# Loads pinned, stores on another queue, two units made earlier and slots shifted in a one-core hybrid layer

## The chip, the cores and the metric

The kernel runs on one core of one Trainium2 chip. The metric is the device time of one execution in microseconds (us). Matrix products run on TensorE (PE in the profile, its weight loads PEld), element-wise work on VectorE (DVE) and ScalarE (ACT), a little of it on GpSimd (POOL). SyncE (SP) only issues DMAs. ScalarE and GpSimd issue DMAs too. An engine runs its instructions, DMA issues among them, in one fixed order, and a waiting instruction holds up all that stand behind it.

## The reference

One decoder layer on 512 tokens of width 2048, with 16 meta tokens ahead of them, in float32:

```
u = rmsnorm(h, norm_mix);  proj = u @ w_in
mix = concat(attention(proj), mlstm(proj) * gate)
h = h + mix @ w_out                                     # 2048 x 2048
u = rmsnorm(h, norm_mlp)
h = h + square(relu(u @ w_up)) @ w_down                 # 2048 x 8192, 8192 x 2048
return rmsnorm(h, norm_final)
```

The change lies in the last column block of `w_out`, in the product with `w_up` and at the start of the product with `w_down`.

## The kernel before, in words

**Split products.** Each float32 operand is split into a high half in fp32r and the remainder. ScalarE makes the high half (the cast at L121), VectorE subtracts it from the source (L122), and TensorE takes three products: high x high, high x low, low x high. In the names, `whi` and `wlo` are the halves of a weight (three buffers each), and tiles `s0` to `s15` of `xpool` are slots that hold high and low halves of activations side by side. A slot is 2 x 528 numbers wide (`TOK` is 528). `xpair(i, 512)` uses 2 x 512 of them, from the slot's start if `i` is even and 32 numbers (128 bytes) later if it is odd.

**w_out (L838 to L914).** Four blocks of 512 columns, j = 0 to 3. For each, four 1 MB weight tiles come through two buffers (`raw_tile`, L134), 512-row products run at L714 to L716, VectorE adds the residual rows (`hs`, L869), the rows are stored to DRAM (`hd`, L873), transposed by TensorE (L878) and turned into the seven combinations of rows that the next product uses. Their squares are summed by ScalarE (L707). The rows tile has two buffers, so blocks 2 and 3 use one each.

**w_up (`up_quad`, L746 to L834).** The product is done in 32 quads of hidden units by a fast 2x2 scheme with seven products instead of eight. A quad loads two 1 MB raw tiles (L753): even quads into the two buffers of `raw_tile`, odd quads into two buffers of a pool `b2r` that lies where the tiles of the w_out loop were. `x11`, `x12`, `x21`, `x22` are its quarters. VectorE makes the sums s1 to s4 (L744, three buffers, `NS_`), `operand` splits a quarter or a sum, and `product` runs 24 matmuls (8 blocks of k, three each, L764 to L766) for it. From quad 1 on the order of products is x11, x12, s2, s1, s3, s4, x22. The activations of the scheme are `yh[p, j]`, `yl[p, j]`: for j below 2 in tiles of their own (`y`), for j = 2 and 3 in slots 0 to 13 (two for each p). Quad 0 is begun inside the last block of w_out by `first_quad`. At the end of a quad come square, four sums `fs` (L829 to L832, on VectorE, for the last quad on GpSimd) and two stores to `fdram` (L833, L834).

**w_down (from L986).** It reads the activations back as 512-number "units" (`load_unit`, L950), in the order of `keys_`, and splits each into a slot (`split_unit`): unit k goes to slot `XU[k]`, so units 0 and 1 go to slots 14 and 15, which w_up leaves free, and units 2 and 3 to slots 0 and 1, which hold rows of the first product. Units 0 and 1 are made early, in quads 4 and 5 (`early_unit`). `load_units` and `next_units` keep five loads ahead (`FB`). The products (L1068 to L1072) run in 16 blocks of 14 steps of 12 matmuls. A step needs its weight operand, its units and now and then a difference of weight tiles (`weight_sum`, L1037).

**Order.** Tile's scheduler orders each engine's instructions by a simulation of the program. Inside `manual_schedule` (for w_down: TensorE, ScalarE and VectorE) the written order is kept. Before its first product w_down writes: operands 0 and 1, the first half of `t1`, and `next_units(3)`, so units 2, 3 and 4. Then step 0: the second half of `t1`, operand 2, one unit.

Of the kernel before, what the change touches and what calls it, by code (L numbers as in the profile page):

```python
# [11 lines left out]
F32R = mybir.dt.float32r  # L12
# [5 lines left out]
P = 128  # L18
# [5 lines left out]
TOK = META + SEQ  # L24
# [15 lines left out]
NQ = FF // P // 2  # L40
HTOK = SEQ // 2
NS_ = 3
FB = 5
# [40 lines left out]
def hybrid_layer(ctx, tc, io, out):  # L84
# [15 lines left out]
        return aps.tile(list(shape), F32, tag="a", name="a")  # L100


    def xpair(i, n, dt=F32R):
        t = xpool.tile([P, 2 * TOK], dt, tag=f"s{i}", name=f"s{i}")
        o = (TOK - n) * (i % 2) * 2
        return t[:, o : o + 2 * n].rearrange("p (a n) -> p a n", a=2)

    cst = cpool.tile([P, C_N], F32, name="cst")
    act.dma_start(out=cst[:, :KT], in_=io["cst"][:, :KT])
# [613 lines left out]
    b2 = b2s.enter_context(tc.tile_pool(name="b2", bufs=1, reuse_waits="tile"))  # L723
    yh, yl = {}, {}

    def y_pair(p, j, t):
        t = t.rearrange("p a (q n) -> p a q n", q=2)
        yh[p, j], yl[p, j] = t[:, 0], t[:, 1]

    for p in ORDER:  # L730
        for j in range(2):
            y_pair(p, j, b2.tile([P, 2, 512], F32R, name=f"y{p}_{j}")[:])

    def sum_tile():
        return b2.tile([P, 1024], F32, name="s", tag="s", bufs=NS_)


    def operand(src):
        w = hi_lo()
        split(w[0][:], w[1][:], src)  # L740
        return w
# [4 lines left out]
    def up_quad(quad):  # L746
        raws = []
        for i in range(2):
            if quad % 2:
                raw = b2r.tile([P, 2048], F32, name=f"raw{i}")  # L750
            else:
                raw = raw_tile()
            sync.dma_start(out=raw[:], in_=io["w3"][quad, i])  # L753
            raws.append(raw)
        x11, x12 = raws[0][:, :1024], raws[0][:, 1024:]
        x22, x21 = raws[1][:, :1024], raws[1][:, 1024:]
        s1, s2, s3, s4 = (sum_tile() for _ in range(4))
        nb = abank if quad % 2 else bank

        def product(p, w, out, q0=0, q1=KQ, start=True):  # L760
            for q in range(q0, q1):
                wh, wl = (t[:, q * P : (q + 1) * P] for t in w)
                ah_, al_ = yh[p, q // 2][:, q % 2], yl[p, q // 2][:, q % 2]
                pe.matmul(out, wh, ah_, start=start and q == 0, stop=False, skip_group_check=True)  # L764
                pe.matmul(out, wh, al_, start=False, stop=False, skip_group_check=True)  # L765
                pe.matmul(out, wl, ah_, start=False, stop=q == KQ - 1, skip_group_check=True)  # L766

        if quad == 0:
            pa, pb, pc = (nb((P, 2, HTOK)) for _ in range(3))
            pd = nb((P, HTOK))  # L770
            pp2, pp6 = pd[:], pa[:, 1]
            w_sum(s1, x21, x22, ALU.add)
            w_sum(s2, s1[:], x11, ALU.subtract)
            w_sum(s4, x12, s2[:], ALU.subtract)
            early = [(p, operand(src), o) for p, src, o in ((0, x11, pa[:, 0]), (1, x12, pp2), (2, s4[:], pc[:, 1]))]
            yield
            product(*early[0], 0, 2)
            yield
            for (p, w, o), q0 in zip(early, (2, 0, 0)):
                product(p, w, o, q0, KQ - 2)  # L780
            yield
            for p, w, o in early:
                product(p, w, o, KQ - 2, KQ)
            product(4, operand(s1[:]), pb[:, 1])
            product(3, operand(x22), pc[:, 0])
            w_sum(s3, x11, x21, ALU.subtract)
            product(6, operand(s3[:]), pb[:, 0])
            product(5, operand(s2[:]), pp6)

            d = b2b.tile([P, 4, HTOK], F32, name="d", bufs=2)  # L790
            v = b2b.tile([P, 4, HTOK], F32, name="fs")
            sb, u2, u = v[:, 2], v[:, 3], v[:, :2]
            act.copy(sb, pa[:, 0])
            dve.tensor_tensor(out=d[:, 0], in0=sb, in1=pp2, op=ALU.add)
            dve.tensor_tensor(out=u2, in0=sb, in1=pp6, op=ALU.add)
            dve.tensor_tensor(out=u, in0=v[:, 3:].to_broadcast([P, 2, HTOK]), in1=pb[:], op=ALU.add)
            dve.tensor_tensor(out=d[:, 3], in0=u[:, 0], in1=pb[:, 1], op=ALU.add)
            dve.tensor_tensor(out=d[:, 1:3], in0=u, in1=pc[:], op=ALU.add)
            act.activation(d[:], d[:], AF.Relu)
        else:  # L800

            X, B = nb((P, HTOK)), nb((P, 2, HTOK))
            W, Q = B[:, 0], B[:, 1]
            d = b2b.tile([P, 4, HTOK], F32, name="d", bufs=2)
            product(0, operand(x11), X[:])
            act.copy(d[:, 0], X[:])
            w_sum(s1, x21, x22, ALU.add)
            w_sum(s2, s1[:], x11, ALU.subtract)
            product(1, operand(x12), W)
            product(5, operand(s2[:]), X[:], start=False)  # L810
            dve.tensor_tensor(out=d[:, 0], in0=d[:, 0], in1=W, op=ALU.add)  # L811
            act.copy(d[:, 2], X[:])
            product(4, operand(s1[:]), Q)
            w_sum(s3, x11, x21, ALU.subtract)
            act.copy(d[:, 1], Q)
            product(6, operand(s3[:]), X[:], start=False)
            w_sum(s4, x12, s2[:], ALU.subtract)
            act.copy(d[:, 3], X[:])
            product(2, operand(s4[:]), Q, start=False)
            dve.tensor_tensor(out=d[:, 3], in0=d[:, 3], in1=d[:, 1], op=ALU.add)  # L820
            act.activation(d[:, 0], d[:, 0], AF.Relu)
            product(3, operand(x22), X[:], start=False)
            dve.tensor_tensor(out=d[:, 2], in0=d[:, 2], in1=Q, op=ALU.add)
            act.activation(d[:, 2:4], d[:, 2:4], AF.Relu)
            act.activation(d[:, 1], X[:], AF.Relu)
        act.activation(d[:], d[:], AF.Square)
        fs = b2b.tile([P, 4, HTOK], F32, name="fs")
        summer = dve if quad < NQ - 1 else pool
        summer.tensor_tensor(out=fs[:, 0], in0=d[:, 2], in1=d[:, 3], op=ALU.add)  # L829
        summer.tensor_tensor(out=fs[:, 1], in0=fs[:, 0], in1=d[:, 0], op=ALU.subtract)  # L830
        summer.tensor_tensor(out=fs[:, 2], in0=d[:, 2], in1=d[:, 0], op=ALU.subtract)
        summer.tensor_tensor(out=fs[:, 3], in0=d[:, 1], in1=fs[:, 1], op=ALU.subtract)  # L832
        act.dma_start(out=fdram[quad // 2][0][:, :, quad % 2], in_=d[:])  # L833
        (act if quad < NQ - 1 else pool).dma_start(out=fdram[quad // 2][1][:, :, quad % 2], in_=fs[:])  # L834
# [3 lines left out]
    with tc.tile_pool(name="b2a", bufs=1, reuse_waits="tile") as b2a:  # L838
        for j in range(NJ):
# [30 lines left out]
                        out=hs[b][:], in0=ps[b][:], scalar=sc[:, b : b + 1], in1=hs[b][:], op0=ALU.mult, op1=ALU.add  # L870
                    )
            for b in range(NB):
                sync.dma_start(out=hd[j][b // 2][:, b % 2], in_=hs[b][:])  # L873
            ts = [abank((P, NB, P)) for _ in range(4)]

            def transposes(i, bs):
# [18 lines left out]
                act.activation(y[:, i], src, AF.Copy, scale=gmlp[:, kt : kt + 1])  # L895
            if j >= 2:
                for i, p in enumerate(ORDER):
                    y_pair(p, j, xpair(2 * i + j - 2, 512))
            y11, y12 = y[:, 0:2, :HTOK], y[:, 0:2, HTOK:]
            y21, y22 = y[:, 2:4, :HTOK], y[:, 2:4, HTOK:]  # L900
            t1, t2, t4 = (b2a.tile([P, 2, HTOK], F32, name=f"t{i}")[:] for i in range(3))
# [45 lines left out]
    def load_unit(k, buf):  # L947
        c, p, h = keys_[k]
        pos = FPOS.index(p)
        sync.dma_start(out=buf[:].rearrange("p (a b) -> p a b", a=2), in_=fdram[2 * c + h][pos // 4][:, pos % 4])  # L950

    def split_unit(k, buf):
        unit[keys_[k]] = hi, lo = unit_pair(k)
        split(hi, lo, buf[:])
# [42 lines left out]
    def load_units(n):  # L997
        for k in range(len(loaded), min(n, len(keys_))):
            loaded[k] = f_buffer()
            load_unit(k, loaded[k])  # L1000

    def next_units(n):
        for k in range(len(unit), min(len(unit) + n, len(keys_))):
            load_units(k + FB)
            split_unit(k, loaded[k])
# [191 lines left out]
        last_sq[b] = b3.tile([P, 1], F32, name=f"sq{b}")  # L1197
        act.activation(junk, h1[b, j], AF.Square, accum_out=last_sq[b][:])

    load_units(FB)  # L1200
    load_rows0(0, 0)
    load_rows0(0, 1)
    load_rows1(0)
# [1 line left out]
    with tc.manual_schedule(engines={mybir.EngineType.PE, mybir.EngineType.Activation, mybir.EngineType.DVE}):  # L1205
        weight_operand(0)
        weight_operand(1)
        weight_sum(0, "t1", 0)
        next_units(3)
        for g in range(LAST):  # L1210
            product(g)
            step(g)
            if g == LAST - STEPS + 2:
                load_nf()
            elif g == LAST - STEPS + 8:
                for j in range(NJ):
                    act.activation(nfs[j][:], nfs[j][:], AF.Copy, scale=float(D) ** 0.5)

        for row, j in ((0, 3), (1, 2)):
            b = slice(2 * row, 2 * row + 2)  # L1220
            pool.tensor_scalar(out=ssh[:, b, j], in0=epss[:, b], scalar1=float(D), scalar2=None, op0=ALU.mult)
        for m in range(STEPS - 2):
            product(LAST + m)
            last_step(m)
# [89 lines left out]
```

## Time and profile before

| | |
|---|---|
| median of three runs | 1988.95 us (1987.78 to 1991.22) |
| the profiled execution | 1988.79 us, its span 1987.0 us |
| granted TensorE clock, mean | 0.997 |
| bytes read from and written to HBM | 244.45 MB, 78.15 MB |

The profile is of one execution. Its span goes from the first to the last instruction. Times of day in the text are microseconds from the span's start. In a row of a timeline stand start, duration, engine, line, operation, tile written and tiles read, shapes and count; in brackets follows how long the engine had been idle before it and what ended that. Rows close together and alike are merged, so that a duration can be that of several. The rows of TensorE overlap, since matmuls are pipelined: the distance of their starts tells the pace.

### The profile page before, as it was taken

How to read it: one execution, taken by the hardware profiler on the slowest of the kernel's cores; microseconds unless marked ns; L12 is line 12 of the kernel's file. 1: busy time of each engine (PE TensorE's matmuls, PEld its weight loads, DVE VectorE, ACT ScalarE, POOL GpSimd, SP SyncE). 2: the span in 40 equal slices, each digit the busy share in tenths (PEclk: the TensorE clock that was granted, in tenths of full speed). 3: DMA queues.
4: the chain of work that ended last, by engine and by line, in shares of the span. 5: the costliest groups of instructions: out<-in, count | busy, mean ns of one | idle time of the engine just before them, and what ended most of it. 6: DMA issues, size and time to landing. Idle time of an engine off the chain costs nothing.

```text
span 1987.0 us, 30628 instructions
## 1 busy us (share of the span) xinstructions
PE 1964.6 (99%) x12240; PEld 1759.7 (89%) x12240; DVE 1407.7 (71%) x1844; ACT 1011.8 (51%) x1491; POOL 226.0 (11%) x342
## 2 busy tenths in 40 slices
PE   9999999999999999999999999999999999999997
PEld 7878889988888889999999999998888888888885
DVE  6547773233644478777777787778898898888888
ACT  4433542235533355555555555556566666655655
POOL 0112220012120021222210000001100010010010
PEclk9999999999999999999999999999999999999999
DMA  8412112211343346555554454547888887787866
GB/s 315 132 64 87 64 65 86 85 69 64 107 155 139 107 148 215 180 188 175 186 180 160 149 170 149 170 149 230 225 223 213 232 216 211 227 216 201 220 173 189
DMA packets 113008, 324.61 MB, mean 163 GB/s; under 512 B 14016, under 2 KB 50496, under 8 KB 93904
## 3 DMA queue, kind: packets, MB, share of 16 engines
q1 hardware_dynamic: 66304, 246.60, 36.5%
q0 software_dynamic: 12000, 40.90, 10.7%
q10 hardware_dynamic: 34560, 35.14, 5.5%
q8 instruction: 96, 1.57, 0.3%
q14 instruction: 48, 0.39, 0.1%
HBM read 244.45 MB, written 78.15 MB: 162 GB/s over the span
## 4 chain that ended last, share of the span: by engine, by line
PE 68%; issue 24%; POOL 3%; DVE 2%; DMA 2%; ACT 1%; SPq 0%; POOLq 0%; DVEq 0%; ACTq 0%
PE g L168 10%; PE a L766 5%; PE a L765 5%; PE a L764 5%; PE g L764 5%; PE g L765 5%; PE g L766 5%; PE g L714 3%; PE g L716 3%; PE g L715 3%; PE g L231 2%; PE g L183 2%; POOL hd L1078 2%; PE g L181 2%; PE g L182 2%
## 5 line engine op out<-in xcount | busy, mean ns | idle before, releaser
L121 ACT CAST whi<-raw 128x1024 fp32r<-128x1024 f32 x224 | 234.9, 1049 | 409.1 <-PE g L716 85.5
L122 DVE TENSOR_TENSOR wlo<-raw,whi 128x1024 fp32r<-128x1024 f32 x224 | 274.7, 1227 | 206.4 <-ACT whi L121 201.4
L122 DVE TENSOR_TENSOR wlo<-s,whi 128x1024 fp32r<-128x1024 f32 x256 | 313.4, 1225 | 119.9 <-ACT whi L121 117.6
L121 ACT CAST whi<-s 128x1024 fp32r<-128x1024 f32 x256 | 268.9, 1051 | 223.1 <-PE a L765 67.1
L168 PE MATMUL g<-s,whi 128*128 128x264 f32 x1216 | 205.0, 287 | 0.2 <-DVE qa L267 0.2
L168 PEld LDWEIGHTS g<-s,whi 128*128 128x128 f32 x1216 | 170.9, 189 | 5.4 <-issue 4.9
L1068 PE MATMUL X<-whi,s 128*128 128x512 f32 x356 | 138.5, 389 | 0.0
L1071 PE MATMUL X<-wlo,s 128*128 128x512 f32 x356 | 138.5, 389 | 0.0
L1072 PE MATMUL X<-whi,s 128*128 128x512 f32 x356 | 138.5, 389 | 0.0
L764 PE MATMUL g<-y,whi 128*128 128x256 f32 x448 | 127.2, 284 | 1.3 <-ACT whi L121 1.1
L764 PE MATMUL a<-y,whi 128*128 128x256 f32 x448 | 127.0, 284 | 1.5 <-DVE d L811 1.0
L168 PE MATMUL g<-s,wlo 128*128 128x264 f32 x608 | 128.0, 287 | 0.0
L766 PE MATMUL a<-y,wlo 128*128 128x256 f32 x448 | 127.0, 283 | 0.6 <-DVE wlo L122 0.6
L764 PE MATMUL a<-s,whi 128*128 128x256 f32 x448 | 126.8, 283 | 0.0
L765 PE MATMUL a<-s,whi 128*128 128x256 f32 x448 | 126.8, 283 | 0.0
L766 PE MATMUL a<-s,wlo 128*128 128x256 f32 x448 | 126.8, 283 | 0.0
L766 PE MATMUL g<-y,wlo 128*128 128x256 f32 x448 | 126.8, 283 | 0.0
L765 PE MATMUL g<-y,whi 128*128 128x256 f32 x448 | 126.8, 283 | 0.0
L765 PE MATMUL a<-y,whi 128*128 128x256 f32 x448 | 126.8, 283 | 0.0
L765 PE MATMUL g<-s,whi 128*128 128x256 f32 x448 | 126.7, 283 | 0.0
L766 PE MATMUL g<-s,wlo 128*128 128x256 f32 x448 | 126.7, 283 | 0.0
L764 PE MATMUL g<-s,whi 128*128 128x256 f32 x448 | 126.5, 283 | 0.0
(368 smaller groups left out, 5114.4 us busy)
## 6 DMA issues: line engine op xcount, KB each, us to landing
raw<-in_w_dram SPq DMA_DIRECT2D x144, 1024.0 KB, 5.1
rh<-in_w_dram SPq DMA_DIRECT2D x64, 512.0 KB, 5.6
hd<-c POOLq DMA_DIRECT2D x61, 512.0 KB, 5.5
fu<-fd SPq DMA_DIRECT2D x110, 256.0 KB, 3.7
fd<-d ACTq DMA_DIRECT2D x32, 512.0 KB, 3.2
fd<-fs ACTq DMA_DIRECT2D x31, 512.0 KB, 3.5
xtok<-in_x_dram SPq DMA_DIRECT2D x4, 1024.0 KB, 11.6
hs<-in_x_dram SPq DMA_DIRECT2D x16, 256.0 KB, 6.1
```

What stands on the lines that cost most here:

```text
L121: act.copy(dst_hi, src)
L122: dve.tensor_tensor(out=dst_lo, in0=src, in1=dst_hi.bitcast(F32), op=ALU.subtract)
L168: pe.matmul(ps[s][:], w, x[:, s * HALF : (s + 1) * HALF], start=first and kt == 0, stop=last and kt == KT - 1,)
L714: pe.matmul(ps[b][:], a, wh, start=kt == first, stop=False)
L715: pe.matmul(ps[b][:], a, wl, start=False, stop=False)
L716: pe.matmul(ps[b][:], c, wh, start=False, stop=kt == last)
L764: pe.matmul(out, wh, ah_, start=start and q == 0, stop=False, skip_group_check=True)
L765: pe.matmul(out, wh, al_, start=False, stop=False, skip_group_check=True)
L766: pe.matmul(out, wl, ah_, start=False, stop=q == KQ - 1, skip_group_check=True)
L1068: pe.matmul(out[:, t], a, wh[:, cols], start=start and h == q == 0, stop=False, skip_group_check=True)
L1071: pe.matmul(out[:, t], a, wl[:, cols], start=False, stop=False, skip_group_check=True)
L1072: pe.matmul(out[:, t], a2, wh[:, cols], start=False, stop=h == q == 1, skip_group_check=True)
```

## The change

- `xslot` returns a whole slot, and `y_pair` takes the first 1024 numbers of a tile. The w_up rows (j = 2, 3) in odd slots therefore start at the slot's start instead of 128 bytes later. Units keep `xpair`.
- In quad 2 both raw loads are kept in program order on SyncE, so they are issued behind everything that the program has put on that queue before, quad 1's loads among it.
- The row stores of the last block of w_out (four of 256 KB) are issued by GpSimd instead of SyncE.
- In the last quad (31) a tile `u` of the sum tiles' ring takes the loads of units 2 and 3, and the two are split behind the second product in the program's text. w_down starts with four units made: it loads units 4 to 8 ahead, and makes one unit (4) instead of three before its first product.

```diff
+    def xslot(i, dt=F32R):
+        return xpool.tile([P, 2 * TOK], dt, tag=f"s{i}", name=f"s{i}")
+
     def xpair(i, n, dt=F32R):
-        t = xpool.tile([P, 2 * TOK], dt, tag=f"s{i}", name=f"s{i}")
         o = (TOK - n) * (i % 2) * 2
-        return t[:, o : o + 2 * n].rearrange("p (a n) -> p a n", a=2)
+        return xslot(i, dt)[:, o : o + 2 * n].rearrange("p (a n) -> p a n", a=2)
...
-    def y_pair(p, j, t):
-        t = t.rearrange("p a (q n) -> p a q n", q=2)
+    def y_pair(p, j, t, o=0):
+        t = t[:, o : o + 1024].rearrange("p (a q n) -> p a q n", a=2, q=2)
         yh[p, j], yl[p, j] = t[:, 0], t[:, 1]
...
-            y_pair(p, j, b2.tile([P, 2, 512], F32R, name=f"y{p}_{j}")[:])
+            y_pair(p, j, b2.tile([P, 1024], F32R, name=f"y{p}_{j}"))
...
-            sync.dma_start(out=raw[:], in_=io["w3"][quad, i])
+            load = sync.dma_start(out=raw[:], in_=io["w3"][quad, i])
+            if quad == 2:
+                tc.keep_in_program_order(load)
...
+        if quad == NQ - 1:
+
+            u = sum_tile()
+            for h in range(2):
+                k = len(loaded)
+                loaded[k] = u[:, h * 512 : (h + 1) * 512]
+                load_unit(k, loaded[k])
         s1, s2, s3, s4 = (sum_tile() for _ in range(4))
...
             product(1, operand(x12), W)
+            if quad == NQ - 1:
+                for k in (2, 3):
+                    split_unit(k, loaded[k])
             product(5, operand(s2[:]), X[:], start=False)
...
-                sync.dma_start(out=hd[j][b // 2][:, b % 2], in_=hs[b][:])
+                (pool if j == NJ - 1 else sync).dma_start(out=hd[j][b // 2][:, b % 2], in_=hs[b][:])
...
-                    y_pair(p, j, xpair(2 * i + j - 2, 512))
+                    y_pair(p, j, xslot(2 * i + j - 2))
...
-    load_units(FB)
+    load_units(4 + FB)
...
-        next_units(3)
+        next_units(1)
```

## The prediction

> **What bounds the kernel now.** I read the page first, then TensorE's own waits, then busy time by stretches, then the timelines of the two places that these point to.
>
> ```profile
> span 1987.0 us, 30628 instructions
> ...
> PE 1964.6 (99%) x12240; PEld 1759.7 (89%) x12240; DVE 1407.7 (71%) x1844; ACT 1011.8 (51%) x1491; POOL 226.0 (11%) x342
> ```
>
> ```profile
> PE W L1071 <- DVE wlo L122: 2.4, 1, 2.4
> ...
> PE g L764 <- ACT whi L121: 1.1, 1, 1.1
> PE a L764 <- DVE d L811: 1.0, 1, 1.0
> ...
> PE a L766 <- DVE wlo L122: 0.6, 1, 0.6
> ```
>
> TensorE is the bound, with 1964.6 of 1987.0 us busy, and no other engine is above 71%. An edit that removes no matmul can win only what TensorE idles and what it runs at a lower clock. The change removes no matmul. The long waits are few: one of 2.4 us in the w_down product (L1071), and a group of about a microsecond each in the w_up products (L764 to L766). What these places really cost is seen by stretches (columns: span, busy time of PE, PEld, DVE, ACT and POOL with counts, granted clock, DMA share, GB/s):
>
> ```profile
> 731.00:742.00 11.00, 8.91 (x68) 8.12 (x67) 11.00 (x14) 6.58 (x9) 3.23 (x4) 1.00 0.11 38
> 742.00:760.00 18.00, 18.00 (x153) 18.00 (x152) 15.99 (x21) 9.49 (x14) 4.10 (x5) 1.00 0.65 219
> 1340.00:1360.00 20.00, 20.00 (x169) 20.00 (x168) 12.62 (x16) 10.73 (x15) 0.00 (x0) 1.00 0.73 226
> ...
> 1365.00:1368.00 3.00, 0.88 (x4) 0.38 (x2) 3.00 (x3) 2.15 (x3) 1.77 (x2) 1.00 0.88 112
> 1368.00:1372.00 4.00, 3.70 (x10) 2.94 (x11) 4.00 (x6) 1.57 (x2) 0.00 (x0) 0.57 0.98 352
> 1372.00:1400.00 28.00, 28.00 (x125) 23.19 (x124) 25.41 (x26) 16.51 (x20) 1.76 (x2) 1.00 0.83 257
> ```
>
> Undisturbed, a w_up matmul takes 18.00 / 153 = 0.118 us and a w_down matmul 28.00 / 125 = 0.224 us. In 731 to 742 us, where the second quad begins, 68 matmuls should take 8.0 us and took 11.0: **3.0 us lost**, with DVE busy all the time. At the passage from w_up to w_down:
>
> ```profile
> 1365.49 0.39 PE L1068 MATMUL W<-whi,s 128*128 128x512 f32 x1
> 1368.30 0.79 PE L1071 MATMUL W<-wlo,s 128*128 128x512 f32 x1 [2.42 <-DVE wlo L122]
> ...
> 1371.44 0.39 PE L1072 MATMUL W<-whi,s 128*128 128x512 f32 x1
> ```
>
> Eight matmuls start from 1365.49 until 1371.44, which is 5.95 us where 8 x 0.224 = 1.79 would do: **4.16 us lost**. Of that 2.42 is the wait, and the other 1.74 is the clock: it was granted at 0.57 over the 4.00 us that follow, and 0.43 x 4.00 = 1.72. Together 7.2 us are to be had in the two places, 0.36% of the run.
>
> **Part 1: the third quad's loads behind the second's, row stores by GpSimd.** Quads are counted from 0, so the third is quad 2. Four loads of L753 matter, in this order on SyncE: both of quad 2 (they reuse quad 0's buffers), then both of quad 1. The last three follow each other at 721.24:
>
> ```profile
> 721.24 1.40 SPq L753 DMA_DIRECT2D raw<-in_w_dram  x3
> ```
>
> ```profile
> SPq L753 <- DVE wlo L122: 8.9, 1, 8.9
> ```
>
> ```profile
> L753 SPq DMA_DIRECT2D raw<-in_w_dram x1: 333/333/333, 721.2 to 721.2; - x1
> ...
> DMA to landing us min/median/max: 4.9/4.9/4.9
> ```
>
> ```profile
> L753 SPq DMA_DIRECT2D raw<-in_w_dram x1: 425/425/425, 721.6 to 721.6; - x1
> ...
> DMA to landing us min/median/max: 8.2/8.2/8.2
> ```
>
> ```profile
> L753 SPq DMA_DIRECT2D raw<-in_w_dram x1: 328/328/328, 722.3 to 722.3; - x1
> ...
> DMA to landing us min/median/max: 10.2/10.2/10.2
> ```
>
> The wait of 8.9 us is quad 2's second load waiting for the last low half made from quad 0's buffer. Behind it stand quad 1's two loads, issued at 721.6 and 722.3, which land at 729.8 and 732.5. The first needs only the buffer of the third column block's residual rows, whose last reader is a square sum:
>
> ```profile
> 699.68 0.18 ACT L707 ACTIVATION_READ_ACCUMULATOR y<-hs 128x1 f32 x1
> ```
>
> ```profile
> 729.92 2.00 ACT L121 CAST whi<-raw 128x1024 fp32r<-128x1024 f32 x2 [5.81 <-DMA raw<-in_w_dram]
> ```
>
> ```profile
> 731.00 2.36 DVE L122 TENSOR_TENSOR wlo<-raw,whi 128x1024 fp32r<-128x1024 f32 x2 [5.09 <-ACT whi L121]
> ...
> 733.94 1.22 DVE L744 TENSOR_TENSOR s<-raw 128x1024 f32<-128x1024 f32 x1
> ```
>
> With the pin, that load can go out from 699.9 and lands some 20 us before 729.92. ScalarE's 5.81 us of waiting for it go, and the two low halves (2.36 us) fall into VectorE's 5.09 us of idleness. Quad 1's second load stays at about 722.3, since its buffer is read by the square sums of the last block until then, but it is first in the queue instead of third: I take the 4.9 us of the load that was first, so 727.2 instead of 732.5. The sum of 733.94 (1.22 us) then moves ahead too. VectorE is 2.4 to 3.6 us ahead where TensorE lost 3.0. So the part is worth **-3.0 us**, with 2.4 if the second load still lands at 732.5, and 0 at worst. Quad 2's own loads now leave from 722.6 and 722.9 and land by about 734, over ten microseconds ahead of the quad they serve.
>
> ```profile
> 707.09 3.62 SPq L873 DMA_DIRECT2D hd<-hs  x4
> ```
>
> ```profile
> 744.59 0.59 POOL L982 DMA_DIRECT2D hd<-res  x1 [0.30 <-POOL res L979]
> ```
>
> The four stores leave SyncE free for 3.62 us and cost GpSimd 4 x 0.59 = 2.4 us, behind which stands only its normalisation after 722. They must have landed by 722.3 to delay no load. Even at 707.1 + 2.4 with 10.2 us to land, the longest above, that is 719.7: **0**.
>
> **Part 2: units 2 and 3 made in the last quad.** On VectorE, in its written order, between the last quad and the low half that L1071 waits for:
>
> ```profile
> 1362.30 3.13 DVE L122 TENSOR_TENSOR s<-fu,s 128x512 fp32r<-128x512 f32 x3 [1.64 <-ACT s L121]
> 1365.35 1.76 DVE L1037 TENSOR_TENSOR s<-raw 128x1024 f32<-128x1024 f32 x1
> 1367.03 1.21 DVE L122 TENSOR_TENSOR wlo<-rh,whi 128x1024 fp32r<-128x1024 f32 x1
> 1368.17 0.68 DVE L122 TENSOR_TENSOR s<-fu,s 128x512 fp32r<-128x512 f32 x1
> ```
>
> ```profile
> 1361.85 0.73 POOL L829 TENSOR_TENSOR fs<-d 128x256 f32<-128x256 f32 x1 [328.96 <-ACT d L826]
> ...
> 1364.95 1.07 POOL L832 TENSOR_TENSOR fs<-d,fs 128x256 f32<-128x256 f32 x1
> ```
>
> The three low halves are units 2, 3 and 4. They take 1.04 us each here and 0.68 at 1368.17: GpSimd's four sums, 1361.85 to 1366.02, slow VectorE by a factor of 1.53, and the weight sum too (1.76 against 1.22). With two units gone, unit 4 ends near 1363.2. The weight sum takes 1.22 x 1.53 = 1.87, to 1365.05. The low half then does 0.97 / 1.53 = 0.63 of its 1.21 us until GpSimd is done and ends at 1366.6. TensorE wants it at 1365.49 + 0.224 = 1365.71. So a gap of 0.9 us stays. For the next two steps VectorE has a sum, a low half and a unit (1.22 + 1.21 + 0.68 = 3.11, some 0.2 less as their ends overlap) against twelve matmuls (2.69): 0.4 more together. The gaps of 1.1 and 1.0 us in w_up left the clock at 1.00, so I let the clock stay. Lost then 1.3 instead of 4.16: **-2.9 us**, between -1.1 (the clock drops again) and -4.16 (nothing late).
>
> The Trainium skill, "SBUF — State Buffer" (Who interferes with whom), says that a VectorE instruction with two SBUF inputs and a GpSimd instruction that reads SBUF exclude each other, the later one waiting for the whole of the other. The slowed rows agree that they hinder each other; by the rule the low half could be held to 1366.02 and end at 1367.2, leaving a gap of 1.5 us and a total 0.6 us higher.
>
> ```profile
> 1345.34 6.29 SPq L1021 DMA_DIRECT2D rh<-in_w_dram  x4
> ```
>
> The loads move too. Units 2 and 3 are loaded as soon as a sum buffer of quad 30 is free, and units 7 and 8 now stand on SyncE ahead of w_down's second weight rows, which went out from 1345.34 for the low half of 1367.03. Two loads of 256 KB at the 226 GB/s of 1340 to 1360 are 2.3 us, hidden by that distance: **0**.
>
> In the last quad the two splits add 2 x 0.68 to VectorE, busy 12.62 of 20.00 us there, and two short casts to ScalarE, busy 10.73: **0**, or 0.5 if a cast queues ahead of one that TensorE needs. If that cover were gone they would cost what they cost now.
>
> **Part 3: slots.** Rows of w_up in the slots (s) and in tiles of their own (y) stream alike, so 128 bytes change nothing: **0**.
>
> ```profile
> L765 PE MATMUL a<-s,whi 128*128 128x256 f32 x448 | 126.8, 283 | 0.0
> ...
> L765 PE MATMUL a<-y,whi 128*128 128x256 f32 x448 | 126.8, 283 | 0.0
> ```
>
> **Sum.** -3.0 - 2.9 = -5.9 us. The profiled execution took 1988.79 us (span 1987.0), 0.16 below the median of the runs, so it stands for them: 1988.95 - 5.9 = 1983.0. After 1372 TensorE runs without gaps, so nothing there takes the gain back.
>
> **Rivals.** A measurement of this kernel can tell about 0.2%, 4.0 us, from no change; the bound is 1985.0.
>
> *The clock drops again.* The gap of 0.9 to 1.5 us lies between one that left the clock alone (1.1) and one that didn't (2.42). It would give back 1.74: 1984.8, on the bound. The Trainium skill, "TensorE: Matmul & The Clock Gate" (What's actually happening), lets the clock fall after an idle window of about 3.4 us; by that neither gap should lower it, and the 2.42 us one did, so the measurement decides.
>
> *Only the passage gains.* The order on TensorE and VectorE in the first quads comes from the scheduler's simulation; if it puts a matmul early whose operand is late, as at the 1.1 us wait of quad 0, the 3.0 us come back in another place: 1986.1.
>
> *Nothing gained.* VectorE is late in both places anyway (11.00 of 11.00 us and 3.00 of 3.00 us busy): 1989.
>
> *Quad 0's wait goes as well*, since SyncE and the order around it change: another 1.1, 1981.9.
>
> *Slower: the ring of sum buffers.* The loads of units 2 and 3 take one of three sum buffers; quad 31's fourth operand (s3) must now wait for their splits.
>
> ```profile
> 1331.78 1.22 DVE L744 TENSOR_TENSOR s<-raw,raw 128x1024 f32<-128x1024 f32 x1
> ```
>
> ```profile
> 1351.38 0.28 PE L764 MATMUL a<-y,whi 128*128 128x256 f32 x1
> ```
>
> The sum is made at 1331.78 now; its product starts at 1351.38. Sum, cast and low half are 1.22 + 1.00 + 1.21 = 3.4 us, so it decides from where unit 3's split ends after 1348.0. Were the splits left where they are now, at 1362.30 to 1364.4, that product would start at 1367.8: 16.4 us, less 5.9, gives 1999.5. Against it: the slots are free after the first product, and both engines idle over a third of that stretch.
>
> **How the numbers follow.** Forecast 0.50; clock 0.12, half on either side of the bound; passage alone 0.17; nothing 0.10; quad 0 too 0.06; slower 0.05. Faster 0.50 + 0.06 + 0.06 = 0.62, same 0.06 + 0.17 + 0.10 = 0.33, slower 0.05. The range goes from 1980.7 (both places whole, 7.2, and quad 0's 1.1) to 1987.9 (the passage alone with its least gain, 1.1), leaving out the slower case and the one without gain.
>
> **What would show it.** Right: quad 1's loads issued ahead of quad 2's, the first before 712; no waits of TensorE at quad 1's first products; stores of the last block on GpSimd; two splits in quad 31; one unit instead of three before the first weight sum; a gap at L1071 near 1 us with the clock at 1.00. Wrong: a wait of ScalarE for a load in quads 1 or 2, a gap above 2 us in the passage, or a wait before quad 31's fifth product.

## The result, and the profile after

| | before | after |
|---|---|---|
| median of six runs, us | 1989.03 (1987.78 to 1991.22) | 1977.47 (1976.87 to 1979.19) |
| ratio, 95% interval | | 0.9941 [0.9929, 0.9954] |
| the profiled execution, span, us | 1988.79, 1987.0 | 1977.64, 1975.9 |

The kernel became 11.6 us faster. The forecast of 1983.0 had the side right, but the time lies below its whole range of 1980.7 to 1987.9: a gain of 5.9 us, as large as the forecast one, came from a place where nothing was expected.

The head of the page of after:

```profile
span 1975.9 us, 30625 instructions
...
PE 1956.7 (99%) x12240; PEld 1752.5 (89%) x12240; DVE 1406.9 (71%) x1844; ACT 1013.2 (51%) x1491; POOL 239.6 (12%) x346
```

Each kernel has 12240 matmuls, and TensorE is busy for 7.9 us less (1964.6 to 1956.7). Had only waits gone, the busy time would have stayed but for the 1.7 us of the low clock. TensorE's longest waits of after (line, what it waited for: total, times, longest):

```profile
PE a L396 <- POOL pr L389: 1.4, 5, 0.4
PE g L196 <- DVE rb L254: 1.2, 1, 1.2
PE W L1085 <- DVE wlo L124: 1.1, 2, 0.7
PE g L775 <- ACT whi L123: 1.1, 1, 1.1
```

The 2.4 us of the passage have become two waits of 1.1 together, the group at quad 1's start is gone, and quad 0's 1.1 (now at L775) stays. The five short waits at L396 lie in attention, where before has three of 1.0 together. By stretches (columns as above), for the same two places:

```profile
731.00:742.00 11.00, 11.00 (x95) 11.00 (x94) 11.00 (x14) 6.28 (x9) 2.15 (x4) 1.00 0.22 83
742.00:760.00 18.00, 18.00 (x154) 18.00 (x153) 13.80 (x20) 9.94 (x13) 8.26 (x4) 1.00 0.69 228
1356.00:1359.00 3.00, 2.30 (x11) 1.59 (x10) 3.00 (x4) 1.72 (x3) 2.62 (x3) 1.00 0.92 219
1359.00:1363.00 4.00, 3.61 (x17) 2.64 (x16) 4.00 (x5) 1.57 (x2) 0.45 (x1) 1.00 1.01 414
```

In 731 to 742 us 95 matmuls run where 68 ran. In the passage, which now lies at 1356 to 1363, the clock stays at 1.00.

**Where the 11.1 us of span went.** The same matmul, counted from the first, is looked up in both traces, and its start of before is taken from its start of after:

| up to | after minus before, us | this stretch |
|---|---|---|
| the end of attention | +0.86 | +0.86 |
| quad 3's first product | -3.30 | -4.16 |
| the end of w_up | -8.71 | -5.41 |
| the passage into w_down | -11.04 | -2.33 |
| the end | -11.04 | 0 |

The second and fourth rows are the two places of the forecast. The third row has no place: there is no wait in it, and the difference grows by 0.187 us in every quad. A quad takes 20.160 us before and 19.973 after; over the 31.5 quads of w_up's whole length that is 5.9 us, of which some 0.5 lies in the second row. The rows of single matmuls show it. Before:

```profile
1000.26 0.28 PE L766 MATMUL g<-y,wlo 128*128 128x256 f32 x1
1000.38 0.28 PE L764 MATMUL g<-y,whi 128*128 128x256 f32 x1
1000.50 0.28 PE L765 MATMUL g<-y,whi 128*128 128x256 f32 x1
1000.62 0.28 PE L766 MATMUL g<-y,wlo 128*128 128x256 f32 x1
```

After, where one product ends in rows of the slots (s) and the next begins in rows of their own tiles (y):

```profile
1000.25 0.28 PE L777 MATMUL g<-s,wlo 128*128 128x256 f32 x1
1000.37 0.28 PE L775 MATMUL g<-y,whi 128*128 128x256 f32 x1
1000.48 0.27 PE L776 MATMUL g<-y,whi 128*128 128x256 f32 x1
1000.60 0.28 PE L777 MATMUL g<-y,wlo 128*128 128x256 f32 x1
1000.71 0.28 PE L775 MATMUL g<-y,whi 128*128 128x256 f32 x1
```

Before, starts stand 0.120 apart (5333 of 5374 distances are exactly 120 ns). After, some are 0.11. In the second column of a row, the duration, there is next to nothing to see. A product of 24 matmuls is 27 ns shorter. The blocks of k that gain are the two whose rows lie in odd slots (6.5 ns in their six matmuls, 118.9 in the mean) and the first of the product that follows (20 ns in ten matmuls, though their rows lie where they lay before).

**A measure of pace.** A count of matmuls in a stretch without waits needs no single rows. Before, 900 to 1300 us (w_up) and 1450 to 1850 us (w_down):

```profile
900.00:1300.00 400.00, 400.00 (x3335) 400.00 (x3335) 307.81 (x357) 211.40 (x298) 30.56 (x41) 1.00 0.50 167
1450.00:1850.00 400.00, 400.00 (x1767) 331.31 (x1766) 353.87 (x344) 243.82 (x282) 35.25 (x41) 1.00 0.81 218
```

After:

```profile
900.00:1300.00 400.00, 400.00 (x3367) 400.00 (x3366) 310.42 (x362) 214.53 (x300) 30.57 (x41) 1.00 0.50 168
1450.00:1850.00 400.00, 400.00 (x1766) 331.35 (x1765) 354.53 (x343) 243.14 (x280) 36.40 (x43) 1.00 0.82 219
```

So 400 / 3335 = 0.1199 us against 400 / 3367 = 0.1188 in w_up, and 0.2264 in w_down both times. Such a count takes in the two matmuls or so that were already running when the window began; by the distance of starts it is 0.1200, 0.1189 and 0.2267. In a short window the two weigh more: the prediction's 18.00 / 153 = 0.118 is too quick a pace for before by more than all that the slots changed. TensorE is busy for all of the 400 us, at clock 1.00, in every kernel: "busy" tells nothing of this.

### The profile page after: what moved, and what is told of

It reads as the page before. It is cut to its first block, busy times and chain, and to the rows that moved or that the text cites. A ratio compares the mean times of both kernels' runs of the same rounds, so it can differ in the third digit from the quotient of the medians.

```text
span 1975.9 us, 30625 instructions
## 1 busy us (share of the span) xinstructions
PE 1956.7 (99%) x12240; PEld 1752.5 (89%) x12240; DVE 1406.9 (71%) x1844; ACT 1013.2 (51%) x1491; POOL 239.6 (12%) x346
## 3 DMA queue, kind: packets, MB, share of 16 engines
q8 instruction: 96, 1.57, 0.3%
## 4 chain that ended last, share of the span: by engine, by line
PE 69%; issue 24%; POOL 3%; DVE 2%; ACT 1%; DMA 1%; POOLq 0%; SPq 0%; DVEq 0%; ACTq 0%
PE g L170 10%; PE a L775 5%; PE g L775 5%; PE a L777 5%; PE a L776 5%; PE g L777 5%; PE g L776 5%; PE g L716 3%; PE g L718 3%; PE g L717 3%; PE g L233 2%; PE g L185 2%; POOL hd L1092 2%; PE g L183 2%; PE g L184 2%
## 5 line engine op out<-in xcount | busy, mean ns | idle before, releaser
L775 PE MATMUL g<-y,whi 128*128 128x256 f32 x448 | 126.3, 282 | 1.1 <-ACT whi L123 1.1
L775 PE MATMUL a<-s,whi 128*128 128x256 f32 x448 | 126.6, 282 | 0.0
L775 PE MATMUL g<-s,whi 128*128 128x256 f32 x448 | 126.2, 282 | 0.0
L775 PE MATMUL a<-y,whi 128*128 128x256 f32 x448 | 125.9, 281 | 0.0
```

## The experiments

**What could set the pace.** Theory A: what counts is the distance, modulo 256 bytes, between where the moving rows and where the stationary weights start in a partition. Tiles `y` and the weight tiles are 4096 bytes, 16 x 256; a slot is 2 x 528 x 4 = 4224 bytes, 16.5 x 256. So each second slot begins half a step off, and the 128 bytes that `xpair` adds in odd slots put its rows back in step. By these sizes, all rows of before are level with each other and with the weights ("level" and "off" are meant so from here on); after, the rows in odd slots are 128 bytes off. The rival: another part of the change makes the steady gain, and the slots make none, as the prediction had it. Quads and single distances below are taken from the traces as above.

### Each part alone

The change of the slots alone, put into the kernel before:

```diff
-    y_pair(p, j, xpair(2 * i + j - 2, 512))
+    y_pair(p, j, xslot(2 * i + j - 2))
```

> The kernel before, with nothing changed but the rows of w_up in odd slots 128 bytes off. Theory A: the pace of the w_up matmuls hangs on where the rows of the moving operand start; so a quad takes 19.97 us instead of 20.16, as in the changed kernel, and the run is 5.9 us (31.5 quads of 0.187 us) faster than before, near 1983, with the waits at 731 to 742 and at 1365 as before. Theory B: the pace came with the new order of loads and of work; then a quad stays at 20.16 us and the run at 1989.

Measured: 1984.21 us against 1989.47, ratio 0.9972 [0.9962, 0.9983].

```profile
900.00:1300.00 400.00, 400.00 (x3367) 400.00 (x3366) 310.45 (x361) 214.86 (x301) 29.48 (x39) 1.00 0.49 167
```

The count is that of after, to the matmul, and quads take 19.97 us, while the waits of before at quad 1 and in the passage are still there. The rival falls.

The change without the slots:

```diff
-    y_pair(p, j, xslot(2 * i + j - 2))
+    y_pair(p, j, xpair(2 * i + j - 2, 512))
```

> The changed kernel without the shift of the rows in odd slots. Theory A: a quad takes 20.16 us again, the gains of the loads and of the units stay, 3.7 + 2.3 = 6.0 us: near 1983. Theory B: a quad stays at 19.97 us and the run near 1977.5.

Measured: 1983.40, ratio 0.9971 [0.9959, 0.9983], quads of 20.16 us. Without the slots the kernel lies within 0.4 us of the forecast of 1983.0.

The pinned loads and the row stores on GpSimd alone, put into the kernel before:

```diff
+            load = sync.dma_start(out=raw[:], in_=io["w3"][quad, i])
+            if quad == 2:
+                tc.keep_in_program_order(load)
...
+    (pool if j == NJ - 1 else sync).dma_start(out=hd[j][b // 2][:, b % 2], in_=hs[b][:])
```

> The kernel before with the third quad's loads behind the second's and the last block's row stores on GpSimd, nothing else. Theory A and the prediction: the waits of 731 to 742 go and nothing else changes, 3 to 4 us faster, near 1985.5, quads at 20.16 us. Theory B: quads at 19.97 us from here on, 9 us faster, near 1980.

Measured: 1986.02, ratio 0.9983 [0.9974, 0.9992], 3.45 us below the kernel before. Its single waits of TensorE of 1 us and more, and one of quad 2 further down the list:

```profile
PE W L1073 <- DVE wlo L122: 2.4, 1, 2.4
PE g L194 <- DVE rb L252: 1.2, 1, 1.2
PE g L766 <- ACT whi L121: 1.1, 1, 1.1
...
PE g L766 <- ACT d L817: 0.3, 1, 0.3
```

Quad 1's are gone and the passage has kept its own. In its trace the difference to before goes from +0.37 to -2.81 at quad 1, so 3.2 us. The last line is a wait that before has too:

```profile
PE g L764 <- ACT d L815: 0.3, 1, 0.3
```

It costs 0.4 us by the distance of starts. It is absent from after and from the runs with the slots alone, without the slots and with the units alone, so it doesn't hang on the loads.

Units 2 and 3 in the last quad alone, put into the kernel before:

```diff
+            if quad == NQ - 1:
+                for k in (2, 3):
+                    split_unit(k, loaded[k])
...
-    load_units(FB)
+    load_units(4 + FB)
...
-        next_units(3)
+        next_units(1)
```

> The kernel before with units 2 and 3 made in the last quad, nothing else. Theory A and the prediction: the 4.2 us lost at the passage to w_down shrink to 1 to 2, so 2.3 to 2.9 us faster, near 1986.5, quads at 20.16 us, clock at full there. Theory B asks nothing else of this run. If the units gain nothing alone, the passage was helped by the earlier start of the quads.

Measured: 1987.79, ratio 0.999 [0.9981, 1.0], so 1.7 us, hardly told from no change. Its waits at L1081 are 1.1 us together, as in after, and in its trace the passage gains the 2.3 us that it gains in after. But its profiled execution lost something elsewhere, in quad 1, which this kernel doesn't touch:

```profile
731.00:740.00 9.00, 7.57 (x57) 6.78 (x55) 9.00 (x12) 4.58 (x7) 3.00 (x4) 1.00 0.10 32
740.00:744.00 4.00, 3.44 (x18) 3.44 (x18) 4.00 (x5) 2.01 (x3) 1.94 (x2) 0.57 0.27 94
```

Here the clock fell at 740.11, within the second of quad 1's waits (1.06 and 0.57 us), which left it alone in before. And with the slots alone, the gap of the passage is the same as in before, and the clock stayed:

```profile
1361.86 0.50 PE L1073 MATMUL W<-wlo,s 128*128 128x512 f32 x1 [2.43 <-DVE wlo L124]
```

```profile
1361.00:1365.00 4.00, 3.14 (x13) 2.44 (x14) 4.00 (x5) 1.42 (x2) 0.00 (x0) 1.00 0.95 307
```

The 1.74 us of the clock is therefore not bound to the gap at L1071 (see the end). The three parts alone give 5.26 + 3.45 + 1.68 = 10.4 us in medians, the whole 11.6.

### What about the slots it is

Even slots off in place of odd ones, and then all fourteen (both from after, one run each; the last argument is `y_pair`'s shift, in numbers of 4 bytes):

```diff
-    y_pair(p, j, xslot(2 * i + j - 2))
+    y_pair(p, j, xslot(2 * i + j - 2), 32)                  # even slots off
+    y_pair(p, j, xslot(2 * i + j - 2), 32 * (1 - j % 2))    # both off
```

> The changed kernel with the shift turned round: w_up's rows in even slots (blocks of k 4 and 5 of a product) lie 128 bytes off the step of 256 bytes on which the weights and all other rows start, those in odd slots (6 and 7) on it. Two theories of the pace. Change-over: a product gains 27 ns each time its rows go over to the other step and back, whichever rows those are, so the quads stay at 19.97 us with the short distances moved by two blocks of k. Off the weights' step: each matmul whose rows start on another step than its weights is shorter by itself, 6 of 24 here too, so 19.97 us as well, but with the short distances on blocks 4 and 5 alone. If the quads are at 20.16 us both fall, and it is the odd slots' own place that counts.

Measured: 1977.59 us, quads of 19.973, the shorter distances two blocks of k earlier. It isn't the odd slots but whichever rows are off.

> The changed kernel with w_up's rows in all fourteen slots 128 bytes off the weights' step (12 of a product's 24 matmuls). Change-over: one change and back per product as before, so quads of 19.97 us. Off the weights' step: twice as many short matmuls, 54 ns a product, so quads of 19.78 us and the run 6 us below the changed kernel's.

Measured: 1976.68 us, quads of 19.973 again. Twice as many rows 128 bytes off gain no more, 27 ns in a product and not 54. So theory A, in the form that each row off gains alike, fell. (Here the twelve off matmuls of a product take 119.0 ns in the mean, and level ones behind them gain the other half of the 27 ns.) The second form was that the gain lies in the changes from level rows to others. If so, more changes must gain more. High halves level and low halves 128 bytes off in half of the slots and the other way round in the rest, from after:

```diff
-        yh[p, j], yl[p, j] = t[:, 0], t[:, 1]
+        yh[p, j], yl[p, j] = (
+            t[:, c : c + 512].rearrange("p (q n) -> p q n", q=2) for c in (o, o + 512 + gap)
+        )
...
-    y_pair(p, j, xslot(2 * i + j - 2))
+    y_pair(p, j, xslot(2 * i + j - 2), 0, 32)
```

> The changed kernel with high and low rows of a slot on different steps of 128 bytes (the low half starts 544 numbers in instead of 512), so that from block 4 on the rows of neighbouring matmuls change steps again and again. Off the weights' step: 6 of 24 matmuls are off, as in the changed kernel, so 19.97 us a quad. Change-over: some nine changes a product instead of two; if each gives what the two give now, 13 ns, a product gains over 100 ns and a quad goes below 19.5 us, 14 us or more off the changed kernel's time; at the least it is below 19.97 us.

Measured: 1976.25, ratio 0.9936 [0.9921, 0.9951], quads of 19.926. That is 7 ns more in a product, far less than the 13 ns that the theory has for each change-over added.

A third distance: in after, the tiles `y` of j = 1 put 64 bytes off by a small tile ahead of them.

```diff
-    for p in ORDER:
-        for j in range(2):
+    for j in range(2):
+        for p in ORDER:
             y_pair(p, j, b2.tile([P, 1024], F32R, name=f"y{p}_{j}"))
+        if j == 0:
+            gap = b2.tile([P, 16], F32, name="gap")
+            pool.memset(gap[:], 0.0)
```

> The changed kernel with the tiles of w_up's rows for j = 1 (blocks of k 2 and 3) 64 bytes off the 256-byte step, besides the odd slots' 128. Change-over: four changes a product instead of two, so up to 27 ns more a product, 0.19 us a quad and 6 us a run, if 64 bytes count like 128. Off the weights' step: 12 of 24 matmuls are off, the same 6 us. If only 128 bytes matter, nothing changes and the quads stay at 19.97 us.

Measured: 1974.65, ratio 0.9927 [0.991, 0.9943], quads of 19.873. Now the test that tells change-over from distance: all rows of activations alike, and all 64 bytes off the weights (after without the slots, with a gap between the weights' pool and the slots', which moves all that lies behind it, w_down's units too).

```diff
+    gap = ctx.enter_context(tc.tile_pool(name="gap", bufs=1)).tile([P, 16], F32, name="gap")
...
+    pool.memset(gap[:], 0.0)
```

> The changed kernel without the odd slots' shift, and with 64 bytes of padding behind the weight buffers, so that all rows of w_up (and everything else that lies behind the weights) start 64 bytes off the weights' 256-byte step, alike. Change-over: rows never change their step, so no gain at all, quads of 20.16 us, near 1983. Distance from the weights: the blocks of k 2 and 3 ran at 113.6 to 117.6 ns a matmul in the run before with 64 bytes, so 168 matmuls at that pace make quads of 19.1 to 19.8 us, and the run 6 to 27 us below the changed kernel without the shift, 1977 to 1956.

Measured: 1995.22 us, ratio 1.0024 [1.0001, 1.0046]. Slower, yet w_up is faster than in any kernel so far:

```profile
900.00:1300.00 400.00, 400.00 (x3398) 400.00 (x3398) 314.57 (x368) 216.85 (x304) 33.24 (x44) 1.00 0.50 170
1450.00:1850.00 400.00, 400.00 (x1716) 322.25 (x1716) 343.03 (x333) 237.77 (x275) 34.39 (x40) 1.00 0.80 213
```

In w_up there is no change-over at all, and the pace is 400 / 3398 = 0.1177 us, steadily. So a gain needs no change-over and the distance stands, with a size that depends on it. By the distance of starts it is 117.8 ns at 64 bytes, 118.9 to 119.0 at 128 (six off matmuls in a row in after, twelve with both slots off) and 120 when level. It doesn't explain what level rows gain behind off ones, which is most of the 27 ns in after. In w_down the same gap costs: 400 / 1716 = 0.2331 us instead of 0.2264, 17.5 us over all its blocks; w_out and what lies ahead of it lose another 5.9 against the run without the slots. There the units are the stationary side and 512 columns of weights move; which of the two turns the gain into a loss isn't separated here. One of the ten runs took 1973.44 us and nine took 1994.42 to 1996.7. All ten are one program with the same places in SBUF, so the distance alone can't make the difference of 22 us; nothing on record explains it.

### The price of the same distance in w_down

The units in odd slots 128 bytes off (from after):

```diff
-            t = xpair(XU[k], 512, dt)
+            t = xslot(XU[k], dt)[:, :1024].rearrange("p (a n) -> p a n", a=2)
```

> The changed kernel with w_down's units in odd slots also at the slot's start, 128 bytes off. In w_down the units are the weights of TensorE and the weight tiles stream. Change-over of either operand: w_down's matmul falls below 226.7 ns wherever slots follow each other; at 13 ns a change and two changes for each pair of units some 3 us in all. If only the streamed operand's place counts: w_down as before, 1977.5. Quads stay at 19.97 us.

Measured: 1985.95, ratio 0.9988 [0.9979, 0.9997], so some 8.5 us above after: neither the gain nor the nothing that I expected.

```profile
900.00:1300.00 400.00, 400.00 (x3367) 400.00 (x3366) 310.45 (x362) 214.45 (x301) 31.99 (x41) 1.00 0.50 168
1450.00:1850.00 400.00, 400.00 (x1743) 327.30 (x1742) 349.31 (x339) 240.66 (x278) 34.40 (x40) 1.00 0.81 217
```

w_up is that of after; w_down goes at 0.2295 us, its steps with off units at 0.233, and the level ones between them at 0.2298. So the 128 bytes that gain in w_up's matmuls of 256 columns hurt in w_down's of 512, and `xpair`'s shift is right for the units.

The low halves of the weights 64 bytes off the high ones (from after, a gap between the buffers of `whi` and `wlo`; the rows and units, which lie behind, move with the low halves):

```diff
+        if not gaps:
+            gaps.append(wpool.tile([P, 16], F32, name="gap", bufs=1))
+            pool.memset(gaps[0][:], 0.0)
```

> The changed kernel with 64 bytes of padding between the high and the low weight buffers, so high and low weights lie on different steps, and rows 64 bytes off the high weights but level with the low ones. In w_up the rows keep their relation among themselves. Change-over of rows alone: quads as in the changed kernel, 19.97 us. In w_down the streamed operand now goes high, low, high, so it changes its step with every matmul: by 13 ns a change two thirds of the 2688 matmuls of 226.7 ns get shorter, 24 us at most; if such quick changes cancel, as when high and low rows alternated (0.05 us a quad), nearly nothing, 1 us.

Measured: 2000.26, ratio 1.0061 [1.0045, 1.0078]; a miss for what I expected. In w_up 3393 matmuls run in the 400 us, in w_down 1708 (0.2342 us each): in both runs that move what lies behind the weights, the shift helps in the one place and costs more in the other. The run also tells something of the weights. By the sizes of the tiles, its rows in w_up start at the same places modulo 256 bytes as those of the next run, and only the low halves lie elsewhere: quads take 19.820 us here and 19.767 there. So the weights' place counts, and not the rows' own alone.

### All rows of w_up off, all units level

From after: a 64-byte gap ahead of the tiles `y`, and the rows in the slots 64 bytes further on than after has them, so that odd slots, half a step off in after, are 64 bytes short of the next step. The buffers of the weights and the units stay where they are.

```diff
+    gap = b2.tile([P, 16], F32, name="gap")
+    pool.memset(gap[:], 0.0)
...
-    y_pair(p, j, xslot(2 * i + j - 2))
+    y_pair(p, j, xslot(2 * i + j - 2), 16)
```

> The changed kernel with every row that w_up streams 64 bytes off its weights' 256-byte step (tiles of their own and even slots 64 bytes ahead, odd slots 64 behind) and w_down's units level with the weight tiles as in the kernel before. Distance theory: a matmul of 256 columns takes 117.5 to 117.9 ns at 64 bytes wherever it stands, and one of 512 takes 226.7 when level; so quads of at most 19.80 us, 0.17 less than in the changed kernel, 5.5 us in all, and w_down at its old pace: near 1972, the fastest version here. If 64 bytes behind do not count like 64 ahead, the quarter of the matmuls on odd slots stays at 118.8 to 120 and the gain is 4 us. If the pace came from the changes of step alone, quads go back towards 20.16 us and the run to 1980 or more.

Measured: 1971.52 us (1969.79 to 1973.22), ratio 0.9909 [0.9893, 0.9926], the fastest of all and below after, whose interval it doesn't touch.

```profile
900.00:1300.00 400.00, 400.00 (x3402) 400.00 (x3401) 314.61 (x365) 216.12 (x304) 30.71 (x41) 1.00 0.50 170
1450.00:1850.00 400.00, 400.00 (x1767) 331.20 (x1766) 355.04 (x343) 242.04 (x277) 36.97 (x43) 1.00 0.83 220
```

0.1176 us in w_up and 0.2264 in w_down, as the distance had it: both places at the best pace seen here at once.

## Why the prediction was right in two parts and wrong in one

**Part 1, the loads: right; -3.0 forecast, -3.2 in the trace where it is alone, -3.7 in after (4.16 less the 0.5 of pace), of which 0.4 isn't the loads'.** In both traces the waits of quad 1 gained 3.2 us; the 0.4 is the wait of quad 2, which went in after and stayed with the loads alone. Quad 1's first load goes out at 700.8 (699.9 was forecast as its earliest):

```profile
L755 SPq DMA_DIRECT2D raw<-in_w_dram x1: 328/328/328, 700.8 to 700.8; - x1
...
DMA to landing us min/median/max: 4.7/4.7/4.7
```

The second goes out at 723.2 and lands at 727.9, against 727.2 forecast. In the timeline of VectorE, quad 1's first low half and its first sum stand 3.1 and 2.3 us earlier than before (731.00 and 733.94):

```profile
727.86 1.23 DVE L124 TENSOR_TENSOR wlo<-raw,whi 128x1024 fp32r<-128x1024 f32 x1 [1.08 <-ACT whi L123]
...
731.61 1.22 DVE L746 TENSOR_TENSOR s<-raw 128x1024 f32<-128x1024 f32 x1
```

The stores on GpSimd cost nothing, as forecast; they are all issued in 2.56 us (2.4 forecast), and with the 4.5 us that the slowest took to land they are there by 715.3 at the latest, ahead of the second load:

```profile
708.25 2.56 POOL L887 DMA_DIRECT2D hd<-hs  x4 [66.73 <-DVE hs L883]
```

**Part 2, the units: right in its mechanism, -2.9 forecast, -2.33 in the trace of after.** The splits run in the last quad at 1335.20 and 1337.27, the fourth operand's sum follows, and no product waits, so the slower rival (the ring of sum buffers) didn't come:

```profile
1335.20 0.68 DVE L124 TENSOR_TENSOR s<-s,s 128x512 fp32r<-128x512 f32 x1
...
1337.27 0.69 DVE L124 TENSOR_TENSOR s<-s,s 128x512 fp32r<-128x512 f32 x1
...
1338.20 1.22 DVE L746 TENSOR_TENSOR s<-raw,raw 128x1024 f32<-128x1024 f32 x1
```

In the passage one unit, the weight sum and the low half follow each other on VectorE, and TensorE waits twice:

```profile
1353.61 0.83 DVE L124 TENSOR_TENSOR s<-fu,s 128x512 fp32r<-128x512 f32 x1 [1.60 <-ACT s L123]
1354.37 1.76 DVE L1051 TENSOR_TENSOR s<-raw 128x1024 f32<-128x1024 f32 x1
1356.05 1.76 DVE L124 TENSOR_TENSOR wlo<-rh,whi 128x1024 fp32r<-128x1024 f32 x1
1357.73 1.22 DVE L124 TENSOR_TENSOR s<-fu,s 128x512 fp32r<-128x512 f32 x1
```

```profile
1353.86 1.19 POOL L845 TENSOR_TENSOR fs<-d 128x256 f32<-128x256 f32 x1
1355.01 1.72 POOL L844 TENSOR_TENSOR fs<-fs,d 128x256 f32<-128x256 f32 x1
1356.81 1.59 POOL L846 TENSOR_TENSOR fs<-d,fs 128x256 f32<-128x256 f32 x1
```

```profile
1356.78 0.39 PE L1082 MATMUL W<-whi,s 128*128 128x512 f32 x1
1357.87 0.50 PE L1085 MATMUL W<-wlo,s 128*128 128x512 f32 x1 [0.70 <-DVE wlo L124]
...
1360.49 0.39 PE L1082 MATMUL W<-whi,s 128*128 128x512 f32 x1
1361.27 0.50 PE L1085 MATMUL W<-wlo,s 128*128 128x512 f32 x1 [0.39 <-DVE wlo L124]
```

By the distance of starts, as the prediction counted, the first wait costs 1357.87 - 1356.78 - 0.224 = 0.87 us (0.9 forecast) and the second 1361.27 - 1360.49 - 0.224 = 0.56. With what comes behind them, the first step gains 3.2 on before and the next ones give back 0.8, where 0.4 was forecast: that term is 0.4 of the 0.5 by which the part came out smaller. The low half took 1.76 us and the weight sum as long, against 1.22 each, while GpSimd's last sums ran. The first gap was met with luck in its parts. With the factor of 1.53 the weight sum was put at 1.87 us and the low half at 1.55, so one was 0.1 too long and the other 0.2 too short; in the rows there is no steady slowing. The ends of the rows above (start plus duration) come in turns: VectorE 1354.44, GpSimd 1355.05, VectorE 1356.13, GpSimd 1356.73, VectorE 1357.81, GpSimd 1358.40, VectorE 1358.95. Whatever duration a row shows, it ends 0.55 to 0.61 us after the other engine's last end, or 1.08 where VectorE works on 1024 columns: one instruction of the one engine, then one of the other. The Trainium skill, "SBUF — State Buffer" (Who interferes with whom), has the later of the two engines wait for the whole of the other's instruction, and these rows agree with it. The gap of 1.5 us that the prediction drew from this rule had the order wrong: it let the low half wait for GpSimd's last sum, and here that sum (1.59 us) waited for the low half.

The clock stayed up, as forecast, but the units don't earn its 1.74 us in every profile: with the slots alone and with the loads alone it stayed up over the old gap as well, and with the units alone it fell in quad 1. In medians the units alone are worth 1.7 us, in their trace the passage gains 2.3.

**Part 3, the slots: wrong, 0 forecast, 5.9 us measured.** This is the step that failed: "Rows of w_up in the slots (s) and in tiles of their own (y) stream alike, so 128 bytes change nothing". Two things were wrong in it. The 283 ns in the rows of L765 are durations of pipelined matmuls, which overlap: a matmul is started each 120 ns, and that distance, not the duration, is what w_up's 31.5 quads add up. A change of 1 ns in 120 stands there 168 times in a quad. And the two rows didn't differ in what was to be judged: s and y started on the same step of 256 bytes before, since `xpair`'s 128 bytes made the odd slots level with the rest. Rows that are alike for that very reason can't show what being unlike does. The right treatment would have been bounds on both sides, as for other things that the trace of before doesn't show: 5400 matmuls with an unknown of a nanosecond each are 5.4 us either way, more than the range allowed.

**The sum.** -3.0 and -2.9 for parts 1 and 2 became -3.7 (0.4 of it the wait of quad 2) and -2.3; with the unforecast -5.9, and +0.9 ahead of w_out, where the change does nothing, they are 11.0 of the 11.1 us of span. That the kernel without the slots lies so near 1983.0 is in part luck: the 0.9, the 0.4 and the 0.5 that part 2 fell short stand in no term of the forecast. The statement that only waits and clock could be won, because no matmul is removed, is what made the range too narrow: a TensorE that is 99% busy can still be busy for less.

## What to carry to other kernels

A busy share near 100% doesn't say that the pace is the best one: count the matmuls in a stretch without waits and compare the distance of starts among places of the same shape, not the durations. Where a change moves an operand in SBUF, compute where both operands of the matmul start before pricing it at nothing, and look whether rows that seem to compare the two cases really differ in it. The best distance is not one for all shapes: here 64 bytes off helps in w_up (256 columns) and hurts in w_down (512), so place each phase's operands for itself and measure it.

## What the runs showed of the hardware

**Pace and distance.** Mean distance of starts against the distance of the two operands' starts modulo 256 bytes: 256 columns moving, 120.0 ns level, 117.8 at 64 bytes, 118.9 to 119.0 at 128, and level rows that follow such rows gain too (118.9 ns in the mean over after's 18 level matmuls of a product); 512 columns moving, 226.7 ns level, 233 to 234.4 off. That the operands' places set the pace is shown by moving the rows alone (1971.52 us) and the units alone (1985.95) against after's 1977.47, and that the weights' places count as well by the quads of 19.820 and 19.767. Why level reads cost the short matmuls and spare the long ones stays open, and so does why level rows are quicker for a while behind others, which makes three quarters of what the slots gain in after; the one run in ten at 1973.44 us shows that something else enters too. Quad 2's wait on ScalarE came back with even or both slots off (0.4 and 0.2 us) and in later runs (up to 0.7), which wasn't followed up.

**GpSimd and VectorE.** Where both add or subtract in SBUF, their rows end in turns, and a row's duration holds the wait for the other engine (VectorE 1.76 us instead of 1.22, GpSimd up to 1.72 instead of 0.73).

**Clock.** In every trace the granted clock falls and rises on a grid of 3.41 us (before, it is up for 1361.92 us, 399 times that, then at half for 3.41). Before, the window from 1364.6 to 1368.0 contained 2.14 us of idleness, and the clock was at half for the window behind it. A gap of the same 2.4 us that falls otherwise on the grid did nothing in two other kernels (1.29 us of it in one window with the slots alone, 1.57 with the loads alone), and with the units alone 1.45 us in the window up to 740.11 were enough. So idle time in a window doesn't decide it by itself, and these traces give no threshold. The Trainium skill, "TensorE: Matmul & The Clock Gate" (What's actually happening), has a free-running window of 4096 cycles at 1.2 GHz, 3413 ns, with which the grid agrees; the whole idle window that it asks for before the clock falls is not what these traces show. So a microsecond or two of waiting can cost 1.7 more or nothing, and a comparison of two single profiles should not credit that to an edit. Medians hold some of it too: of the 25 runs of before beside the parts alone, six had a mean granted clock of 0.995 (median 1990.57 us), nine 0.996 (1989.47), nine 0.997 (1988.55) and one 0.998 (1987.76), and five of after's six had 0.998.
